# Turning half of the v tiles with VectorE and short transfer rows in a backbone on one Trainium2 core

## The chip, the cores and the metric

The kernel runs on one core of a Trainium2 chip. A core has four compute engines with a queue of instructions each: TensorE (PE) for matrix products and transposes into PSUM, VectorE (DVE), ScalarE (ACT) and GpSimd (POOL). SyncE (SP) only starts transfers. Sixteen DMA engines carry the transfers of all queues; in the profile those started by SP are queue q1 and those started by ACT are q10. The metric is the device time of one execution in microseconds (us), lower being better. Times are medians of several runs; profiles come from single executions.

## The reference

Two layers over 256 latent and 256 context tokens of width 1024, batch 1, in float32: a Conformer convolution module, then a bidirectional chunkwise mLSTM, each followed by an MLP with squared ReLU. The change lies in the features of the mLSTM:

```python
def mlstm_features(u, w_up, w_conv, b_conv, w_q, w_k, w_v, w_gate, b_gate, w_o, b_o):
    up = u @ w_up
    xm, z = up[..., :MLSTM_INNER], up[..., MLSTM_INNER:]
    xc = jax.nn.silu(dwconv(xm, w_conv) + b_conv)
    q, k, v = xc @ w_q, xc @ w_k, xm @ w_v
    gates = jnp.concatenate([q, k, v], axis=-1) @ w_gate + b_gate
    o = jax.nn.sigmoid(xm @ w_o + b_o)
    return xc, z, q, k, v, gates, o
```

`MLSTM_INNER` is 2048, split over 4 heads of 512. `v` is used twice: in the product with `w_gate`, and later, per head, as the right-hand side of the attention products, where tokens stand on the contracted dimension.

## The kernel before

Activations lie with channels on the 128 partitions and the 512 tokens (256 context, 256 latent) along the row, so a matrix of 2048 channels is sixteen tiles of 128x512. For accuracy every float32 product is done in three passes: a weight and an input are each split into a rounded high part and a low rest (`split`, lines 148-151: ACT casts the high part, `wh`; DVE subtracts it for the low part, `wl`), and `mm3` (lines 179-184) issues high x high, high x low and low x high.

Weights come as 1 MB loads on SP's queue into three buffers `raw` (`raw_load`, lines 141-144), two weight tiles in each. Four pairs of buffers `wh`/`wl` hold split tiles ahead of PE. `gemm_steps` (lines 224-281) walks over pairs of output tiles; after the last product of tile `m` it calls an epilogue.

The stage of v (lines 1207 to 1265) calls `gemm_steps(wv, range(8), xm, T, v_epi)`. The epilogue `v_epi(m, ps)` copies the product from PSUM to a tile `vt` on ACT and puts the rest of the work on a list, `late`; when an even `m` ends, `flush()` first runs what the two tiles before it have left. That rest is `v_out(m, vt)`:

- when `m % 4 == 3`, four gate products (`gate_acc`, line 1211) of that tile and the three before it, into 32 columns of PE each;
- four transposes of 128x128 on PE (line 1232) into a PSUM tile with the tag `ln`, so that tokens come to lie on the partitions;
- a copy from PSUM to a temporary `vk` of the tag `E` on ACT (line 1234), which has four buffers;
- one transfer of `vk` to a DRAM tensor `v_dr[head]`, issued by ACT (line 1235). `v_dr` holds 128 tokens on its first dimension, four blocks of tokens on the second and 512 channels on the third. `raw_load` fetches it back per head, after 1240 us in the profile.

Between the steps of this stage the kernel runs other work: `wgq_step` (lines 764-782) loads a 1 MB block of `wqT` and multiplies it with gate weights into 32 columns of PE (line 772); `ada_n2.step` (lines 408-430) loads a tile `ar` and scales and adds it on DVE (line 425); `xc_load` (lines 1245-1252) loads what the convolution wrote and splits it into `u` and `xc` tiles. After the stage a last `flush()` handles tiles 14 and 15, the pool of the stage is closed, and the products of the queries begin (lines 195 and 196), with `u` and `xc` as inputs and the tag `E` for each tile's sum (`joined`, lines 202-207).

The order of the instructions on each engine is fixed when the kernel is built: a scheduler takes them by priority, which is the order of the program, but lets a ready instruction of an idle engine go ahead. On the chip each engine works through its own list in that order and waits where data isn't there.

Of the kernel before, what the change touches and what calls it, by code (L numbers as in the profile page):

```python
# [14 lines left out]
P = 128  # L15
D = 1024
DT = D // P
E = 2048
# [52 lines left out]
def hybrid_kernel(ctx: ExitStack, tc: tile.TileContext, xT, vecs_d, wdw_d, ada0_w, ada_w, wg_d, pw1a, pw1, pw2, w1_0, w2_0,  # L71
                  w1_1, w2_1, up_x, up_z, wv, wo, bo_d, wk, wq, wqT, wdown, rows_d, out):
    nc = tc.nc
# [10 lines left out]
    def nm(s):  # L84
        uid[0] += 1
        return f"{s}_{uid[0]}"
# [3 lines left out]
    def tmp(tag, dt=F32):  # L90
        return tp.tile([P, T], dt, tag=tag, name=nm(tag), bufs={"E": 4, "S": 2, "L": 2, "F": 1}[tag])
# [8 lines left out]
    def psum(tag="mm"):  # L100
        return pp.tile([P, 512], F32, tag=tag, name=nm(tag), bufs={"mm": 3, "ln": 2, "fl": 1, "cv": 2}[tag])
# [1048 lines left out]
    v_dr = [dp.tile([P, 4, DH], F32, name=f"v_dr{h}") for h in range(H)]  # L1150
# [59 lines left out]
    def gate_acc(j, w, t, last=False):  # L1210
        nc.tensor.matmul(gps[32 * j:32 * j + 32, :], w, t, start=j not in seen, stop=last,
                         tile_position=(0, 32 * j), skip_group_check=True)
        seen.add(j)
# [4 lines left out]
    def v_epi(m, ps):  # L1218
        vt = B("vt").rearrange("p a b -> p (a b)")[:, :T]
        nc.scalar.copy(vt, ps)  # L1220
        vts.append(vt)
        if m % 2 == 0:
            flush()
        late.append(lambda: v_out(m, vt))

    def v_out(m, vt):
        if m % 4 == 3:
            for j in range(4):
                gate_acc(j, wgv[:, m - 3 + j, :], vts[m - 3 + j])
        tr = psum("ln")  # L1230
        for b in range(4):
            nc.tensor.transpose(tr[:, b * P:(b + 1) * P], vt[:, b * P:(b + 1) * P], ident)
        vk = tmp("E")
        nc.scalar.copy(vk, tr)
        nc.scalar.dma_start(v_dr[m // 4][:, :, (m % 4) * P:(m % 4 + 1) * P], vk.rearrange("p (b c) -> p b c", b=4))
# [755 lines left out]
```

## Time and profile before

| | before |
|---|---|
| time, median of 3 runs (lowest to highest) | 1673.76 us (1672.92 to 1674.23) |
| profiled execution: time, span | 1674.57 us, 1672.9 us |
| mean granted clock of PE | 0.998 |
| busy: PE, PE's weight loads, DVE, ACT | 99%, 82%, 62%, 44% of the span |
| stage of v in the trace | about 735 to 927 us |
| transfers from ACT to `v_dr` | 16 of 256 KB, median 4.1 us from issue to landing |
| queue q1 (SP), whole run | 56,080 packets, 285.44 MB, 48.5% of 16 engines |
| queue q10 (ACT), whole run | 17,712 packets, 14.72 MB, 2.6% of 16 engines |

A row of a group or of the timeline gives the line of the kernel, the engine, the operation, and what it writes and reads ("ln<-ident,vt"; numbers of buffers are left out). "x8" is a count, and "[9.75 <-DMA raw<-wv]" is the idle time before the instruction and what ended it. PEld are the weight loads of PE, which run beside its products; ACTq and SPq are the issuing of transfers by those queues. Matmuls are pipelined, so the duration of one is longer than the distance between two.

### The profile page before, as it was taken

What the parts mean: (1) busy time and instruction counts of PE and PEld (TensorE: products, weight loads), DVE (VectorE), ACT (ScalarE), POOL (GpSimd) and SP (SyncE); (2) the same over time, 40 slices, a digit from 0 to 9 for tenths busy, and PEclk for the clock granted to TensorE, in tenths of its full rate; (3) what the DMA queues carried; (4) which work ended last, traced back from release to release, by engine and by line L of the source; (5) the groups of instructions that cost most, each with busy time, mean ns of one, the idle gap of its engine ahead of it and who ended that gap; (6) DMA issues with size and microseconds to landing.
All of it is one profiled execution on the core that took longest, in us unless ns stands there. A gap on an engine that the chain in (4) does not pass through costs nothing. (4 is left out here: it accounts for less than half of the span.)

```text
span 1672.9 us, 22919 instructions
## 1 busy us (share of the span) xinstructions
PE 1660.0 (99%) x8928; PEld 1366.8 (82%) x8928; DVE 1034.3 (62%) x1877; ACT 744.0 (44%) x1196; POOL 14.3 (1%) x64
## 2 busy tenths in 40 slices
PE   9999999999999999999999999999999999999998
PEld 6665898888888998877788899888878888778887
DVE  6555895666635776752143653564389876786677
ACT  4313573232324476652232532442368654555453
POOL 0000000000000000000000000000000000000001
PEclk9999999999999999999999999999999999999999
DMA  9565213444424065556685753455375555675452
GB/s 356 202 215 207 88 71 114 151 135 139 142 101 151 1 210 187 183 195 248 254 271 168 262 175 120 136 205 170 133 246 192 193 210 211 249 272 190 182 186 92
DMA packets 73902, 301.63 MB, mean 180 GB/s; under 512 B 7519, under 2 KB 23683, under 8 KB 43969
## 3 DMA queue, kind: packets, MB, share of 16 engines
q1 hardware_dynamic: 56080, 285.44, 48.5%
q10 hardware_dynamic: 17712, 14.72, 2.6%
q8 instruction: 70, 1.15, 0.3%
q14 instruction: 40, 0.32, 0.1%
HBM read 284.37 MB, written 15.77 MB: 179 GB/s over the span
## 5 line engine op out<-in xcount | busy, mean ns | idle before, releaser
L150 DVE TENSOR_TENSOR wl<-raw,wh 128x1024 fp32r<-128x1024 f32 x344 | 418.7, 1221 | 275.7 <-ACT wh L149 273.2
L149 ACT CAST wh<-raw 128x1024 fp32r<-128x1024 f32 x344 | 359.3, 1052 | 509.6 <-PE mm L183 277.2
L183 PE MATMUL mm<-u,wh 128*128 128x512 f32 (+1 forms) x808 | 291.7, 361 | 0.2 <-DVE u L610 0.2
L180 PE MATMUL mm<-u,wh 128*128 128x512 f32 (+1 forms) x680 | 244.4, 360 | 0.1
L184 PE MATMUL mm<-u,wl 128*128 128x512 f32 (+1 forms) x680 | 241.4, 356 | 0.0
L183 PEld LDWEIGHTS mm<-u,wh 128*128 128x128 f32 x808 | 152.6, 189 | 23.1 <-issue 1.0
L180 PEld LDWEIGHTS mm<-u,wh 128*128 128x128 f32 x680 | 128.5, 189 | 25.7 <-issue 6.4
L184 PEld LDWEIGHTS mm<-u,wl 128*128 128x128 f32 x680 | 128.4, 189 | 18.8 <-issue 1.0
L211 PE MATMUL mm<-wh,xl 128*128 128x512 f32 x256 | 101.1, 395 | 0.0
L180 PE MATMUL mm<-xm,wh 128*128 128x512 f32 x256 | 101.0, 395 | 0.0
L212 PE MATMUL mm<-wh,xl 128*128 128x512 f32 x256 | 100.1, 391 | 0.0
L184 PE MATMUL mm<-xm,wl 128*128 128x512 f32 x256 | 99.7, 390 | 0.0
L213 PE MATMUL mm<-wl,xl 128*128 128x512 f32 x256 | 99.2, 391 | 0.1
L180 PE MATMUL mm<-hid,wh 128*128 128x512 f32 (+1 forms) x256 | 93.3, 364 | 0.0
L183 PE MATMUL mm<-hid,wh 128*128 128x512 f32 (+1 forms) x256 | 92.9, 363 | 0.0
L184 PE MATMUL mm<-hid,wl 128*128 128x512 f32 (+1 forms) x256 | 92.8, 363 | 0.0
L195 PE MATMUL mm<-x,wh 128*128 128x512 f32 x232 | 81.1, 398 | 0.0
L425 DVE SCALAR_TENSOR_TENSOR S<-ar,cs,S 128x512 f32<-128x512 f32 x56 | 40.8, 749 | 59.0 <-DMA ar<-ada_w 58.9
L183 PE MATMUL mm<-qq,wh 128*128 128x272 f32 x256 | 73.9, 289 | 0.0
L180 PE MATMUL mm<-qq,wh 128*128 128x272 f32 x256 | 73.5, 288 | 0.0
L184 PE MATMUL mm<-qq,wl 128*128 128x272 f32 x256 | 73.5, 288 | 0.0
L195 PE MATMUL mm<-u,wh 128*128 128x512 f32 x192 | 68.7, 399 | 0.0
(535 smaller groups left out, 3265.5 us busy)
## 6 DMA issues: line engine op xcount, KB each, us to landing
raw<-w SPq DMA_DIRECT2D x64, 1024.0 KB, 4.8
raw<-wo SPq DMA_DIRECT2D x32, 1024.0 KB, 4.8
raw<-ada_w SPq DMA_DIRECT2D x22, 1024.0 KB, 6.7
ar<-ada_w SPq DMA_DIRECT2D x80, 256.0 KB, 3.7
raw<-wv SPq DMA_DIRECT2D x16, 1024.0 KB, 7.1
raw<-wqT SPq DMA_DIRECT2D x16, 1024.0 KB, 6.2
raw<-wq SPq DMA_DIRECT2D x16, 1024.0 KB, 4.9
raw<-wk SPq DMA_DIRECT2D x16, 1024.0 KB, 4.9
```

The costliest lines, as they stand in the source:

```text
L149: c = nc.scalar.copy(hi, src)
L150: lastsub[0] = nc.vector.tensor_tensor(lo, src, hi.bitcast(F32), op=ALU.subtract).ins
L180: a = nc.tensor.matmul(ps, wh, xh, start=start, stop=False)
L183: nc.tensor.matmul(ps, wh, xl, start=False, stop=False)
L184: lastmm[0] = nc.tensor.matmul(ps, wl, xh, start=False, stop=stop).ins
L195: todo = [lambda s_, e_: nc.tensor.matmul(ps, wh, r[0], start=s_, stop=e_), lambda s_, e_: nc.tensor.matmul(ps[:, :n], wl, r[0][:, :n], st ...
L211: nc.tensor.matmul(ps, xh, wh, start=start, stop=False)
L212: nc.tensor.matmul(ps, xl, wh, start=False, stop=False)
L213: nc.tensor.matmul(ps, xh, wl, start=False, stop=stop)
L425: nc.vector.scalar_tensor_tensor(a, w, c, a, op0=ALU.mult, op1=ALU.add)
```

## The change

For odd `m`, the part of `v_out` behind the gate products is replaced. VectorE transposes `vt` within blocks of 32x32 into `vk`, so that each block is turned but stays at its place in the 4 x 16 grid of blocks. Four transfers issued by ACT, one for each 32 partitions, then write the blocks to where they belong in `v_dr`: each takes 32 partitions with 16 rows of 32 elements, that is 512 rows of 128 bytes, and the second and third dimension on the DRAM side put them at the right token block and quarter. The PSUM tile, the four transposes on PE, the copy on ACT and the one transfer with 512 rows of 512 bytes are not done for these tiles. Even tiles keep them.

```diff
@@ -1227,6 +1227,14 @@
         if m % 4 == 3:
             for j in range(4):
                 gate_acc(j, wgv[:, m - 3 + j, :], vts[m - 3 + j])
+        if m % 2:
+            vk = tmp("E")
+            nc.vector.transpose(vk, vt)
+            for q in range(4):
+                f0 = (m % 4) * P + 32 * q
+                nc.scalar.dma_start(v_dr[m // 4][:, :, f0:f0 + 32].rearrange("(q i) b j -> i b q j", i=32),
+                                    vk[32 * q:32 * q + 32, :].rearrange("i (b q j) -> i b q j", b=4, q=4))
+            return
         tr = psum("ln")
         for b in range(4):
             nc.tensor.transpose(tr[:, b * P:(b + 1) * P], vt[:, b * P:(b + 1) * P], ident)
```

## The prediction

> **What bounds the kernel now.** I read the page first, then the waits of PE alone, then the stretches around the v stage, and only then single instructions.
>
> ```profile
> span 1672.9 us, 22919 instructions
> ## 1 busy us (share of the span) xinstructions
> PE 1660.0 (99%) x8928; PEld 1366.8 (82%) x8928; DVE 1034.3 (62%) x1877; ACT 744.0 (44%) x1196; POOL 14.3 (1%) x64
> ```
>
> ```profile
> PE fl L342 <- DMA raw<-ada_w: 1.1, 2, 0.9
> ...
> PE mm L183 <- DVE u L610: 0.2, 1, 0.2
> ```
>
> These are the first and the last of the seven rows that the view of waits has for PE over the whole run; the longest is 1.1 us, so all seven together are under 8 us. The kernel is one long row of matrix products with hardly a gap. Two things follow. A matmul taken out anywhere shortens the run by the time until the next one could start, because nothing else ends later. And a delay on another engine costs nothing until PE has to wait for it; from then on it costs in full, since PE has no gap in which to catch up.
>
> ```profile
> 735.00:835.00 100.00, 100.00 (x511) 71.90 (x513) 25.05 (x26) 27.80 (x39) 0.00 (x0) 1.00 0.69 252
> 835.00:925.00 90.00, 90.00 (x430) 72.12 (x422) 39.01 (x59) 33.12 (x57) 0.00 (x0) 1.00 0.65 211
> 925.00:950.00 25.00, 25.00 (x141) 20.73 (x139) 15.83 (x28) 13.23 (x27) 0.00 (x0) 1.00 0.87 301
> ```
>
> The columns are length, then busy time of PE, PE's weight loads, DVE, ACT and POOL, then clock, DMA share and GB/s. The first two stretches are the v products, the third the start of the queries. In the v stage DVE and ACT work a quarter to two fifths of the time and the transfers two thirds. In the third stretch everything is fuller: DVE 63%, ACT 53%, transfers 87%. If the change hurts, I expect it there.
>
> **What the change removes from PE.** Sixteen tiles of v are turned, four transposes each; eight tiles lose theirs. They stand in two patterns. Where an even tile of the next group of four ends, the turns of both waiting tiles run together, eight in a row (four such runs; first and last):
>
> ```profile
> 764.99 1.03 PE L1232 MATMUL ln<-ident,vt 128*128 128x128 f32 x8
> 765.95 0.64 PE L772 MATMUL fl<-raw,wgq 128*32 128x512 f32 x4
> ```
>
> ```profile
> 917.44 1.03 PE L1232 MATMUL ln<-ident,vt 128*128 128x128 f32 x8
> 918.23 0.48 PE L180 MATMUL mm<-xm,wh 128*128 128x512 f32 x1
> ```
>
> From the first transpose to the next other instruction it is 0.79 us in the last run, 0.96 in the first, where the 32-column product after it starts later and will go on doing so. I take 0.79: half of it is 0.40 us, four times 1.6 us. In the other four places the gate products stand between the two tiles, and the odd tile's four transposes come behind them (first and last):
>
> ```profile
> 793.37 0.66 PE L1232 MATMUL ln<-ident,vt 128*128 128x128 f32 x4
> 793.95 0.64 PE L772 MATMUL fl<-raw,wgq 128*32 128x512 f32 x4
> ```
>
> ```profile
> 926.70 0.66 PE L1232 MATMUL ln<-ident,vt 128*128 128x128 f32 x4
> 927.11 0.36 PE L196 MATMUL mm<-u,wl 128*128 128x256 f32 x1
> ```
>
> That is 0.58 us once, where two 32-column products will now touch, and 0.41 three times: 1.8 us. The saving on PE is 1.6 + 1.8 = 3.4 us. With 0.96 in place of 0.79 for the two runs that end at a 32-column product it would be 3.6; that is the ceiling, because nothing else leaves PE.
>
> **What it adds elsewhere.** On ACT each odd tile loses one copy and one transfer issue, and gets four issues:
>
> ```profile
> L1234 ACT COPY E<-ln x16: 579/593/610, 768.2 to 927.4; 128x512 f32<-128x512 f32 x16
> ```
>
> ```profile
> L1235 ACTq DMA_DIRECT2D v_dr<-E x16: 520/521/1534, 768.8 to 928.0; - x16
> ```
>
> An old issue names 128 x 4 = 512 rows of 512 bytes, a new one 32 x 16 = 512 rows of 128 bytes, so I price it the same, 0.52 us when nothing disturbs it. Four are 2.1 us; less one copy (0.59) and one issue (0.52) that is 1.0 us more of ACT per odd tile, 8 us in 190. At the longest row, 1.53, it would be 6.1 - 1.1 = 5.0 us. On DVE comes one block transpose per odd tile, which this trace does not show. Nearest are operations over as many elements:
>
> ```profile
> L1198 DVE SCALAR_TENSOR_TENSOR E<-pad,vecs,E 128x512 f32<-128x512 f32 x12 | 9.0, 750 | 9.5 <-ACT E L1196 9.0
> ...
> L421 DVE TENSOR_SCALAR S<-ar,cs 128x512 f32<-128x512 f32 x2 | 1.0, 482 | 2.9 <-DMA ar<-ada_w 2.9
> ```
>
> Between 0.48 and 0.75 us; I take 0.6, as it has one input: 5 us of DVE in a stretch where it is idle for 126 of 190. This goes at nothing.
>
> The transfers: 8 x 512 = 4,096 packets of 512 bytes go, 8 x 2,048 = 16,384 of 128 bytes come. What one costs is read where that queue (q10, ACT's) was nearly alone, from 920 to 922 us, and how it shares with SP's weight loads (q1) from 802 to 804:
>
> ```profile
> q10 hardware_dynamic: 1031, 0.51, 85.2%
> ```
>
> ```profile
> q1 hardware_dynamic: 101, 0.70, 91.9%
> q10 hardware_dynamic: 101, 0.05, 8.5%
> ```
>
> 0.852 x 16 engines x 2 us / 1,031 packets is 26 ns each. By its bytes alone a 128-byte packet would take a quarter, 6.6 ns; I take 26, a price per packet, as the same queue to the same tensor is the nearest row. At 26 the change adds 12,288 x 26 ns / 16 = 20 us of transfer time to 190 us that are two thirds full, at 6.6 nothing. More important is the second pair: with work in both queues they take turns, one packet each, 101 against 101. A weight packet there takes 0.919 x 32 us / 101 = 291 ns, so a small packet in front of each costs the weights 9% at most, as in the run before. The small ones pile up and drain when the weights pause. The Trainium skill ("DMA: Bandwidth & Descriptors", Queues, rings and completion order) says an engine drains a whole packet, typically 9 to 17 descriptors, from one queue before it turns to the next. The equal counts are turns of single records and do not show such bundles; by them an odd tile's small packets, 2.5 us of transfer time at 26 ns, would all go ahead of the weights, and with the later issue (below) a load would be up to 0.7 us late at each of two places: a sum of 2 us in place of 3.4.
>
> **Cover in the middle of the stage.** ACT's casts of the weights stand behind the issues. The tightest place is the first pair:
>
> ```profile
> 768.81 1.31 ACTq L1235 DMA_DIRECT2D v_dr<-E  x2
> 770.16 1.05 ACT L149 CAST wh<-raw 128x1024 fp32r<-128x1024 f32 x1 [0.90 <-ACT E L1234]
> ```
>
> ```profile
> 772.50 0.33 SPq L143 DMA_DIRECT2D raw<-wv  x1
> ```
>
> ```profile
> 781.42 2.37 DVE L150 TENSOR_TENSOR wl<-raw,wh 128x1024 fp32r<-128x1024 f32 x2 [8.96 <-ACT wh L149]
> ```
>
> ```profile
> 786.40 0.39 PE L180 MATMUL mm<-xm,wh 128*128 128x512 f32 x1
> ```
>
> The cast at 770.16 frees the raw buffer for the load at 772.50; when that has landed, its two halves are cast and subtracted from 781.42 on (the first done near 782.6), and PE begins on it at 786.40. That is 3.8 us of cover. Five issues in place of two make the cast 1 to 2 us later; the transfer engines work off what is queued meanwhile, so the landing moves by that or less. Hidden; without cover it would be 1 to 2 us at each of two or three such places.
>
> ```profile
> L149 ACT CAST wh<-raw 128x1024 fp32r<-128x1024 f32 x30 | 30.9, 1050 | 86.3 <-DMA raw<-wv 43.8 <-PE mm L183 35.7 <-DVE S L425 4.4
> ```
>
> The 35.7 us in which these casts wait for PE lie almost all behind 835 us: there they are as far ahead as their four buffers let them, and a delay is hidden. ACT now also waits for DVE's transpose before the four issues, and casts stand behind that on ACT, as subtractions stand behind the transpose on DVE. But vt is there long before the flush, so the transpose can be done early, except for tile 15. Nothing is moved past SP's or POOL's queue.
>
> **Cover at the end of the stage.** Tile 15 has no such lead:
>
> ```profile
> 925.79 0.52 ACTq L1235 DMA_DIRECT2D v_dr<-E  x1
> 927.39 0.59 ACT L1234 COPY E<-ln 128x512 f32<-128x512 f32 x1 [1.63 <-PE ln L1232]
> 927.87 0.41 ACT L149 CAST xc<-raw 128x256 fp32r<-128x256 f32 x1
> 928.00 0.52 ACTq L1235 DMA_DIRECT2D v_dr<-E  x1
> 928.57 2.26 ACT L149 CAST xc<-raw 128x256 fp32r<-128x256 f32 x7 [0.28 <-ACT xc L149]
> ```
>
> ```profile
> 933.91 0.39 PE L195 MATMUL mm<-xc,wh 128*128 128x512 f32 x1
> ```
>
> The last xc cast ends at 930.8; PE takes the first xc at 933.9, so about 3 us of cover. The copy at 927.39 waited for PE's turn; DVE can do its turn earlier. So the four issues, 2.1 us, start about 0.7 us sooner than the one did, the casts end 0.5 to 1 us later, and PE arrives 0.4 us earlier: some 1.5 us of cover stay.
>
> **The sum.** The profiled execution took 1674.57 us, 1.67 around its span of 1672.9, and lies 0.81 above the median of 1673.76. 1674.57 - 3.4 is 1671.2; against the median, 1670.4. A measurement of this kernel tells about 0.2%, 3.35 us, from no change. The forecast lies on that bound.
>
> **The rivals.**
>
> *ACT is held at the end (slower), 0.27.* Tile 14's one and tile 15's four transfers put 5 x 32 = 160 packets on each of the 16 engines. The trace shows that ACT may run ahead of the engines by two: both issues of 768.81 were through at 770.12, and the next row (770 to 772) has no packet of q10 at all.
>
> ```profile
> q1 hardware_dynamic: 107, 0.75, 103.9%
> ```
>
> Whether it may run ahead by five, nothing shows. If 64 is the most, 96 packets per engine must go first, and weight loads keep the engines at 87% there. Taking turns at 291 + 26 ns, that is up to 30 us, in the pauses 2.5; halfway, near 12 us, is where loads dry up because ACT's casts no longer free their buffers. Of 12 us, 3 are covered and 1 replaced: PE waits about 8, net 8 - 3.4, 1678.4 us, and 1674.5 to 1681.5 for a hold of 8 to 15. It decides once ACT is held for over 5 us. Against it: the second of a pair of issues took at most 1.5 us.
>
> *Small rows are dear (slower), 0.13.* If a 128-byte write cost double, 53 ns, the change would add (16,384 x 53 - 4,096 x 26) / 16 = 48 us to the 190, the share would go to 0.92, the small packets would still be queued when the queries start, and the temporary that holds tile 15 would come free late, with ACT's copies of the queries behind it: 5 to 8 us of waits less 3.4, 1676 to 1678. The Trainium skill ("DMA: Bandwidth & Descriptors", Specifications) speaks against the change so: below 512 bytes a transfer engine reads, modifies and writes. No row here has a data row that short.
>
> *Cover runs out here and there (no difference), 0.10.* One to two microseconds at the first and third pair: 1671.5 to 1673.5. For it, the 3.8 us of cover; against it, the turn taking.
>
> **How the numbers follow.** The forecast, all hidden, has 0.50: 1670.4, itself 1669.8 to 1671.4. As 3.4 is so near 3.35 I split it, 0.30 faster and 0.20 within. With the rivals: faster 0.30, same 0.20 + 0.10 = 0.30, slower 0.27 + 0.13 = 0.40. The range from 1669.6 to 1681.0 leaves out the longest holds and a saving above the ceiling, together under 2 in 10.
>
> **What would show it.** Right: 32 transposes of v in place of 64, the pair at 871 replaced by four that take 0.4 us, PE's list of waits unchanged, four issues of about 0.52 us per odd tile, small packets at 7 to 26 ns. Wrong: a PE wait for xc, u or wh between 925 and 945; single issues of 2 us and more; weights that land some microseconds later after their issue than before; or a small packet at 50 ns or above.

## The result and the profile after

| | before | after |
|---|---|---|
| median (lowest to highest), 20 runs each | 1674.39 us (1672.92 to 1676.93) | 1676.90 us (1673.89 to 1679.91) |
| after / before | | 1.0015, 95% interval 1.0009 to 1.0022 |
| profiled execution: time, span | 1674.57, 1672.9 us | 1675.15, 1673.1 us |

The change costs 2.5 us where the forecast had a gain of 3.4. The time lies inside the range that was given, on the other side of no change. By the 0.2% that the prediction took as the least that can be told it would count as no change; over twenty runs each it is clear of noise. The profiled execution of after is one of its quicker ones, so what its trace shows is the lower end of the loss.

The head of the page of after:

```profile
span 1673.1 us, 22872 instructions
## 1 busy us (share of the span) xinstructions
PE 1658.8 (99%) x8896; PEld 1365.2 (82%) x8896; DVE 1038.6 (62%) x1885; ACT 737.1 (44%) x1188; POOL 14.3 (1%) x64
```

PE has 32 matmuls fewer (8896 against 8928), the transposes of eight tiles. They are gone; something gives the time back. The same stretches as before, and the one behind them (columns: length, PE, PE's weight loads, DVE, ACT, POOL, clock, DMA share, GB/s):

```profile
735.00:835.00 100.00, 100.00 (x507) 71.50 (x506) 28.22 (x30) 26.75 (x37) 0.00 (x0) 1.00 0.72 254
835.00:925.00 90.00, 90.00 (x416) 71.50 (x414) 38.42 (x58) 28.08 (x49) 0.00 (x0) 1.00 0.70 213
925.00:950.00 25.00, 24.12 (x135) 20.53 (x135) 19.05 (x33) 15.23 (x31) 0.00 (x0) 1.00 0.81 266
950.00:975.00 25.00, 22.67 (x124) 19.55 (x123) 15.44 (x26) 11.23 (x21) 0.00 (x0) 0.93 0.73 249
```

The stage of v itself is as full as before. PE has gaps only behind 925 us, 0.9 us in the third stretch and 2.3 us in the fourth, and in the fourth the clock is 0.93. PE's list of waits has two rows there that before has not:

```profile
PE mm L195 <- DVE E L206: 2.3, 1, 2.3
...
PE mm L195 <- ACT wh L149: 0.9, 2, 0.5
```

How these come about can be followed back from ACT's timeline at the end of the stage (start, length, line, and in brackets the idle time before):

```profile
922.51 2.67 ACTq L1235 DMA_DIRECT2D v_dr<-E  x4
925.23 0.71 ACT L149 CAST u<-raw 128x256 fp32r<-128x256 f32 x2 [3.10 <-DMA v_dr<-E]
925.85 2.56 ACT L149 CAST xc<-raw 128x256 fp32r<-128x256 f32 x8
928.31 1.04 ACT L149 CAST wh<-raw 128x1024 fp32r<-128x1024 f32 x1
929.25 0.20 ACT L149 CAST qq<-rk 128x16 fp32r<-128x16 f32 x1
929.36 1.04 ACT L149 CAST wh<-raw 128x1024 fp32r<-128x1024 f32 x1
```

Behind tile 15's four issues stand the last two casts of `u`, then those of `xc`, then the casts of the third and fourth tile of query weights. Before, the order was another: all casts of `u` and both of these `wh` stood ahead of tile 15's `vt` copy. The scheduler fixes the lists when the kernel is built, and with four issues where one stood it had ordered the work around them anew. The last cast of `u` before, and what follows it on DVE and on SP:

```profile
923.06 0.41 ACT L149 CAST u<-raw 128x256 fp32r<-128x256 f32 x1 [0.95 <-PE mm L183]
```

```profile
923.50 0.42 DVE L150 TENSOR_TENSOR u<-raw,u 128x256 fp32r<-128x256 f32 x1 [0.20 <-ACT u L149]
```

```profile
923.95 0.33 SPq L143 DMA_DIRECT2D raw<-wq  x1
```

And after:

```profile
925.66 0.76 DVE L150 TENSOR_TENSOR u<-raw,u 128x256 fp32r<-128x256 f32 x2 [3.08 <-ACT u L149]
```

```profile
926.45 0.33 SPq L143 DMA_DIRECT2D raw<-wq  x1
```

In both kernels the third load of query weights is issued 0.03 us behind the end of the last subtraction of `u` (923.92 and 926.42): it goes into the `raw` buffer from which `u` is cast. Tile 15's `vt` copy is at 924.69 before and 920.75 after, so the load goes out 0.7 us ahead of that copy before and 5.7 us behind it after. The larger wait comes 37 us later. VectorE's timeline there, and PE's, both of after:

```profile
962.50 0.75 DVE L425 SCALAR_TENSOR_TENSOR L<-ar,cs,L 128x512 f32<-128x512 f32 x1 [3.96 <-DMA ar<-ada_w]
963.17 0.42 DVE L206 TENSOR_TENSOR E<-mm,E 128x256 f32<-128x256 f32 x1
```

```profile
960.45 0.40 PE L195 MATMUL mm<-u,wh 128*128 128x512 f32 x1
960.68 0.28 PE L196 MATMUL mm<-u,wl 128*128 128x256 f32 x1
960.80 0.40 PE L195 MATMUL mm<-u,wh 128*128 128x512 f32 x1
961.03 0.28 PE L196 MATMUL mm<-u,wl 128*128 128x256 f32 x1
963.64 0.50 PE L195 MATMUL mm<-u,wh 128*128 128x512 f32 x1 [2.33 <-DVE E L206]
...
964.66 0.63 PE L195 MATMUL mm<-u,wh 128*128 128x512 f32 x1
965.09 0.41 PE L196 MATMUL mm<-u,wl 128*128 128x256 f32 x1
965.30 0.63 PE L195 MATMUL mm<-u,wh 128*128 128x512 f32 x1
```

An addition of `ada_n2` (line 425) waits 3.96 us for its tile `ar`; the sum of line 206, which PE needs, stands behind it on DVE, and PE loses 2.33 us. This is the fifth sum of the queries. In DVE's list seven additions of line 425 stand between tile 15's `vt` copy and this sum, and it starts 42.4 us behind that copy; before, five stand there, and it starts 34.5 us behind:

```profile
958.50 0.75 DVE L425 SCALAR_TENSOR_TENSOR L<-ar,cs,L 128x512 f32<-128x512 f32 x1 [1.00 <-DMA ar<-ada_w]
959.17 0.42 DVE L206 TENSOR_TENSOR E<-mm,E 128x256 f32<-128x256 f32 x1
```

After its wait PE runs slower for 3 us: a pair of products takes 0.64 us (964.66 to 965.30) where it took 0.35 before the gap (960.45 to 960.80).

The prices that the prediction had to bound can now be read. The four issues and DVE's turn:

```profile
L1235 ACTq DMA_DIRECT2D v_dr<-E x32: 581/672/4660, 769.9 to 924.5; - x32
```

```profile
L1232 DVE STREAM_TRANSPOSE E<-vt x8: 702/705/711, 769.1 to 921.4; 128x512 f32<-128x512 f32 x8
```

And the queues, from 923 to 925 us, where q10 is alone, and from 826 to 828 us (packets, MB, share of 16 engines):

```profile
q10 hardware_dynamic: 1583, 0.39, 83.8%
```

```profile
q1 hardware_dynamic: 116, 0.84, 99.8%
q10 hardware_dynamic: 115, 0.01, 4.7%
```

0.047 x 32 us / 115 makes 13 ns for a packet of 128 bytes. The Trainium skill ("DMA: Bandwidth & Descriptors", Specifications) has writes below 512 bytes as read, modify and write; here such a packet costs half of what the 512-byte packets cost (26 ns), not more, though by the byte that is twice as much.

### The profile page after: what moved, and what is told of

Its sections match the earlier page's. It is cut to its first block, busy times and chain, and to the rows that moved or that the text cites. A ratio compares the mean times of both kernels' runs of the same rounds, so it can differ in the third digit from the quotient of the medians.

```text
span 1673.1 us, 22872 instructions
## 1 busy us (share of the span) xinstructions
PE 1658.8 (99%) x8896; PEld 1365.2 (82%) x8896; DVE 1038.6 (62%) x1885; ACT 737.1 (44%) x1188; POOL 14.3 (1%) x64
## 4 chain that ended last, share of the span: by engine, by line
PE 94%; DVE 3%; DMA 2%; issue 1%; ACT 0%; ACTq 0%; SPq 0%; DVEq 0%
PE mm L180 17%; PE mm L184 17%; PE mm L183 17%; PE mm L195 6%; PE mm L211 4%; PE mm L213 4%; PE mm L212 4%; PE mm L196 3%; PE cv L211 2%; PE cv L213 2%; PE cv L212 2%; DMA ar<-ada_w 1%; PE fl L342 1%; PE ln L180 1%; PE cv L855 1%; PE ln L183 1%
```

## The experiments

Ratios are to the kernel before, run on the same chip beside it, with 95% intervals. Diffs are against the change unless it says otherwise. The first theories were: L, the loss is the order of ACT's list at the end of the stage; R, short rows slow the weight loads; H, ACT is held by the four issues wherever they stand; D, the transpose on DVE upsets something.

**The change once more.** 

> The change as it is, for a second profile beside the runs below. All theories: ratio 1.0015 (1.0009 to 1.0022). Theory L (order of ACT's list: the casts of the query weights that stood ahead of vt 15 now stand behind tile 15's four issues and the eight xc casts): PE waits of 2 to 7 us, all between 925 and 960 us, on wh or on DVE's sum of the queries. Theory R (128-byte rows slow the weight loads wherever they run): part of PE's waits before 925 us, on wh.

Measured: 1677.06 us, 1.0019 (1.0010 to 1.0028). Its profiled execution took 3.0 us of waiting for the sum of line 206, 2.0 us for `wl` and 0.9 us for `wh`, all between 925 and 970 us.

**One transfer for the four.**

```diff
-            for q in range(4):
-                f0 = (m % 4) * P + 32 * q
-                nc.scalar.dma_start(v_dr[m // 4][:, :, f0:f0 + 32]..., vk[32 * q:32 * q + 32, :]...)
+            nc.scalar.dma_start(v_dr[m // 4][:, :, (m % 4) * P:(m % 4 + 1) * P], vk.rearrange("p (b c) -> p b c", b=4))
```

> VectorE turns the odd tiles, but they are stored with one transfer of 512-byte rows as before (the 128-byte blocks stay at their old place, so v is not the reference's). Removes both the short rows and three of four issues; PE saves its 3.4 us. Theories L and R: 0.998 (-3.4 us), no PE wait between 925 and 960. Theory D (the transpose on DVE itself, or the removal on PE, upsets the order): 1.001 or more.

Measured: 1669.94 us, 0.9978 (0.9969 to 0.9987), no wait of PE between 925 and 975 us. Taking 32 transposes from PE is worth 3.7 us (1673.63 - 1669.94), and VectorE's turn hurts nothing. D falls.

**Transposes left on PE, four transfers for odd tiles** (against the kernel before).

```diff
+        vk3 = vk.rearrange("p (b c) -> p b c", b=4)
+        if m % 2:
+            for q in range(4):
+                f0 = (m % 4) * P + 32 * q
+                nc.scalar.dma_start(v_dr[m // 4][:, :, f0:f0 + 32], vk3[:, :, 32 * q:32 * q + 32])
+            return
```

> TensorE turns all tiles as before, but the odd tiles are stored with four transfers of 512 rows of 128 bytes in place of one. No saving on PE. In its list on ACT the casts of the query weights stand ahead of vt 15 and of tile 15's four issues, as before the change. Theory L: 1.000 (within 1 us of before), although 16,384 short rows move and ACT is held by 32 issues. Theory R: the change's loss of 5.9 us without its saving, 1.0035. Theory H (ACT is held by the issues, wherever its casts stand): 1.002 to 1.004.

Measured: 1675.94 us, 1.0015 (1.0006 to 1.0024), by another way than the change. Here one issue is held for 4.1 us in mid-stage with a cast of weights behind it. The next load of weights is issued when that cast's subtraction has ended, its casts wait 5.8 us for it, and behind them stands the copy of line 777 for which PE waits (ACT's timeline, then SP's, then PE's waits):

```profile
824.37 4.14 ACTq L1239 DMA_DIRECT2D v_dr<-E  x1
828.55 1.05 ACT L149 CAST wh<-raw 128x1024 fp32r<-128x1024 f32 x1 [7.14 <-issue]
...
835.92 1.99 ACT L149 CAST wh<-raw 128x1024 fp32r<-128x1024 f32 x2 [5.83 <-DMA raw<-wv]
837.82 0.58 ACT L777 COPY F<-fl 128x512 f32<-128x512 f32 x1
```

```profile
830.89 0.33 SPq L143 DMA_DIRECT2D raw<-wv  x1
```

```profile
PE fl L780 <- ACT F L777: 1.8, 1, 1.8
```

PE's clock is 0.50 from 840 to 842 us, and eight products from 838.96 to 842.36 us take some 1.5 us more than they do at full clock. So H is not empty: a group of four can cost where something urgent stands behind it. In the change this cast stands ahead of the issues (819.79 us), and its load goes out at 822.13 us.

**The change for tiles 1 to 11 only, and for tiles 13 and 15 only.**

```diff
-        if m % 2:
+        if m % 2 and m < 12:      # first kernel
+        if m % 2 and m > 12:      # second kernel
```

> The change for odd tiles below 12 only; 13 and 15 are turned by TensorE and stored with one transfer. Keeps six of eight turns' saving, 2.6 us, and three quarters of the short rows. Theories L and H (loss at the end of the stage): 0.9985 (-2.6 us). Theory R: loss 4.4 less 2.6, 1.001.

> The change for tiles 13 and 15 only; 0.8 us of saving. Theory L: the whole loss remains, PE waits of 3 to 6 us between 925 and 970: 1.0015 to 1.003. Theory R: a quarter of the loss of 5.9 less 0.8: 1.0004.

Measured: 1671.45 us, 0.9991 (0.9982 to 0.9999) without the last two, with no wait of PE between 925 and 975 us; 1679.65 us, 1.0034 (1.0021 to 1.0048) with them alone, with 4.3 us of waits for the sum and 0.9 for `wh`. All of the loss hangs on tiles 13 and 15; the other six give a gain.

**The four issues at a lower priority of the scheduler.**

```diff
             for q in range(4):
                 f0 = (m % 4) * P + 32 * q
-                nc.scalar.dma_start(...)
+                with tc.high_priority(-400):
+                    nc.scalar.dma_start(...)
```

> The whole change, its four issues per odd tile only given a lower priority, so that the scheduler puts each of them into a later gap of ACT's list: the casts of the query weights stand ahead of vt 15 again. Same instructions, same 128-byte rows, same issues. Theory L (order of ACT's list at the end of the stage): the PE saving shows, 0.998 (-3.5 us), no PE wait between 925 and 970. Theory R (short rows slow the loads): as the change, 1.0015 to 1.002. Theory H (ACT held by the issues, wherever they stand): 1.000 to 1.002.

Measured: 1670.68 us, 0.9980 (0.9972 to 0.9989). The same rows, bytes and issues, only at other places in ACT's list: R falls, and the change is worth what the forecast said, 3.6 us.

**The same four issues with rows of 512 bytes, and the issues on GpSimd's queue.**

```diff
-                nc.scalar.dma_start(v_dr[m // 4][:, :, f0:f0 + 32]..., vk[32 * q:32 * q + 32, :]...)   # short rows
+                nc.scalar.dma_start(v_dr[m // 4][32 * q:32 * q + 32, :, ...], vk[32 * q:32 * q + 32, :]...)  # first kernel
+                nc.gpsimd.dma_start(...)                                                               # second, short rows
```

> VectorE turns the odd tiles; four issues per tile, each of 32 partitions with 512-byte rows (128 rows), so no short rows and issues of about 0.33 us; the blocks stay at their old place, so v is not the reference's. Its list on ACT has one cast of the query weights behind vt 15 and the next behind the xc casts, like the change. Theory L: PE waits on the late cast, between 0.999 and 1.001, above the 0.998 of one transfer. Theories R and H: 0.998.

> The whole change with the four transfers issued by GpSimd in place of ACT. The 128-byte rows all move; ACT is not held and its casts of the query weights stand ahead of vt 15. Theories L and H: 0.998. Theory R: 1.0015 or more. If GpSimd is slow at issuing, tile 15's temporary comes free late and ACT's copies of the queries wait for it: 1.001 to 1.003, with ACT waiting for DMA v_dr.

Measured: 1671.23 us, 0.9982 (0.9973 to 0.9991), and 1671.65 us, 0.9985 (0.9976 to 0.9994). The first missed what I had expected. One of the two casts of query weights stood behind the casts of `xc`, as in the change, and it cost nothing; that put in doubt that these casts are what matters in the order. The issues of this kernel took 0.57 us and more in place of 0.33, so tile 15's four hold ACT for 2.67 us, as in the change. But all casts of `u` stand ahead of them, and the third load of query weights goes out together with tile 15's `vt` copy (920.23 and 920.24 us).

**The casts of query weights late, alone.** In the kernel before, and in the kernel with one transfer per odd tile, a copy of one column makes these two casts wait until they stand as in the change.

```diff
+        if after is not None:
+            nc.vector.tensor_copy(hi[:, 0:1], after)
         anchors.append(split(hi, lo, src))
...
+                late = xcs[12][0][:, 0:1] if w_ap is wq and (g, kh) == (0, 1) else None   # second kernel: vts[15][:, 0:1]
```

> The kernel before, with its transposes on TensorE and its single transfers; only the casts of the third and fourth tile of query weights are made to wait for the first cast of xc (a copy of one column on VectorE writes into their buffer first), so that in ACT's list they stand where the change put them: behind all eight casts of xc, the products of row rk between them. No group of four issues holds ACT. Theory O, the order alone costs: 1.0015 to 1.0035, with waits of PE for wh and, some steps on, for E of L206 between 925 and 970 us. Theory OH, the order costs only together with the two groups of issues that hold ACT for 2.7 us each: 0.9995 to 1.0006, no such waits over 0.5 us.

> Odd tiles turned by VectorE and stored with one transfer of 512-byte rows (v is not the reference's), and the casts of the third and fourth tile of query weights made to wait for tile 15's vt (a copy of one column on VectorE), so that they stand behind the eight casts of xc as in the change. One issue per odd tile in place of four. Theory O: the 4 us that this kernel gained without the late casts are lost again, 0.9998 to 1.0012. Theory OH: 0.9973 to 0.9987, as without the late casts.

Measured: 1674.57 us, 1.0006 (0.9997 to 1.0015), and 1669.44 us, 0.9971 (0.9960 to 0.9982). The second has all the gain although the two casts stand behind `xc` (ACT's timeline), and its third load of query weights goes out early (SP's):

```profile
923.35 2.56 ACT L149 CAST xc<-raw 128x256 fp32r<-128x256 f32 x8 [1.36 <-PE cv L1214]
925.81 1.05 ACT L149 CAST wh<-raw 128x1024 fp32r<-128x1024 f32 x1
```

```profile
920.90 0.33 SPq L143 DMA_DIRECT2D raw<-wq  x1
```

The late casts of query weights, my reading of L up to here, fall as the cause by themselves.

**Only the issues of tiles 13 and 15 at a lower priority, and every tile turned by VectorE.** The text of the first expectation speaks of tile 15 alone, but `m > 12` takes in tile 13 as well: in the trace all eight issues of the two tiles stand one by one, from 916.77 to 946.65 us.

```diff
+                with tc.high_priority(-400 if m > 12 else 0):     # first kernel
-        if m % 2:
+        if True:                                                  # second, with -400 for all issues
```

> The whole change; only the issues of tile 15 are put into ACT's list at a lower priority, those of tiles 1 to 13 stay as in the change with groups that hold ACT for 4.7 to 7.5 us. The casts of the query weights come ahead of the casts of xc again. Theory that all of the loss is at the end of the stage: 0.9974 to 0.9989, as with all issues at low priority. Rival, the holds in mid-stage cost a part: 0.9992 to 1.0008.

> All sixteen tiles turned by VectorE and stored with four transfers of 128-byte rows, all issues at low priority, so that PE has no transposes of v left. If the saving per tile is what the odd tiles gave (3.7 to 4.4 us for eight of them) and everything else stays hidden: 1666 to 1668 us, 0.995 to 0.9965. If doubling the issues to 64 holds ACT where a cast is due, or buffers of tag E come free late because their issues stand late: 0.9975 to 1.001, with waits of PE for wh, vt or u between 740 and 970 us.

Measured: 1670.07 us, 0.9978 (0.9969 to 0.9987), so the place of the issues of tiles 13 and 15 makes the loss, and the six groups of tiles 1 to 11, of which the first three hold ACT for 6.7 to 8.4 us here, none of it. Tile 15's issues alone were not run. And 1667.74 us, 0.9965 (0.9952 to 0.9977): the best of all, 6.1 us for sixteen tiles. It beats both kernels.

**The casts of `u` early, and late.** The first kernel is the change with its issues in place; only the split of `u` tiles 8 to 11 has a higher priority. In the second, one transfer per odd tile, the last two casts of `u` wait for a cast of `xc`.

```diff
+                with tc.high_priority(50 if m0 == 8 else 0):                   # first kernel, in xc_load
+                    split(ts[s][:, LO], ts[s][:, HI], rx[...])
...
+    u_parts = xc_load(8)                                                       # second kernel
+    xc_load(12)
+    u_parts(3, xcs[12][0][:, 0:1])
```

> The whole change, with tile 15's four issues of 2.7 us where the change has them and as many bytes and rows; only the split of u tiles 8 to 11 gets a higher priority, so that the last two casts of u stand ahead of tile 15's issues in ACT's list. Theory U: the loss comes from those two casts, since the third load of query weights goes into the buffer that they read, and waits for it. Then that load is issued at about the time of tile 15's vt copy in place of 5.7 us behind it, PE doesn't wait for E of L206, and the ratio is 0.9973 to 0.9990. Rival Q: the issues hold something else (the casts of xc, which still come behind them): 1.0005 to 1.0028.

> Odd tiles turned by VectorE and stored with one transfer of 512-byte rows (v is not the reference's), which gave 0.9978; here the last two casts of u wait for a cast of xc (a copy of one column on VectorE), so that they stand behind all casts of xc although one issue per tile holds ACT for 0.6 us only. Theory U: the third load of query weights is issued 4 to 7 us later than without, PE waits for E of L206 or wl between 930 and 970 us, and most of the gain is lost: 0.9995 to 1.0025. Rival Q: 0.9973 to 0.9985.

Measured: 1670.95 us, 0.9984 (0.9975 to 0.9993) with `u` early. Tile 15's issues hold ACT even longer here, and `xc` is cast later than in the change, yet all is well (ACT's and SP's timelines of this kernel):

```profile
919.46 1.02 ACT L149 CAST u<-raw 128x256 fp32r<-128x256 f32 x3 [3.59 <-DMA v_dr<-E]
...
922.14 4.68 ACTq L1235 DMA_DIRECT2D v_dr<-E  x4
926.86 2.56 ACT L149 CAST xc<-raw 128x256 fp32r<-128x256 f32 x8 [4.41 <-issue]
```

```profile
921.03 0.33 SPq L143 DMA_DIRECT2D raw<-wq  x1
```

DVE's list has changed with them. Five additions of line 425 stand ahead of the fifth sum in place of seven, and the sum starts 38.0 us behind tile 15's `vt` copy in place of 42.4, early enough for PE:

```profile
956.59 0.75 DVE L425 SCALAR_TENSOR_TENSOR L<-ar,cs,L 128x512 f32<-128x512 f32 x1 [2.89 <-DMA ar<-ada_w]
957.25 1.22 DVE L150 TENSOR_TENSOR wl<-raw,wh 128x1024 fp32r<-128x1024 f32 x1
958.39 0.42 DVE L206 TENSOR_TENSOR E<-mm,E 128x256 f32<-128x256 f32 x1
```

The later loads of query weights do not tell the two kernels apart: the fourth to the eighth go out 9.7, 11.3, 18.2, 23.0 and 27.8 us behind that copy here, and 9.2, 13.8, 18.8, 23.5 and 28.2 us in the change.

With `u` late: 1671.85 us, 0.9991 (0.9982 to 0.9999), less loss than expected. The delay came out smaller than meant, since the third load went out at 923.25 us, 1.4 us behind tile 15's `vt` copy and ahead of the late casts, so into another buffer. Single executions lie between 1670.11 and 1676.29 us; the profiled one, of 1674.78 us, has the change's wait at the change's place:

```profile
PE mm L195 <- DVE E L206: 2.9, 1, 2.9
```

So late casts of `u` can bring that wait without any group of issues, though not in every execution. Six additions stand ahead of the fifth sum here, as many as in the kernel with one transfer. The two medians differ by 0.0013, and their intervals overlap.

**Two buffers for `ar`**, with the change and with the kernel before.

```diff
-            w = adp.tile([P, 512], F32, tag="ar", name=nm("ar"))
+            w = adp.tile([P, 512], F32, tag="ar", name=nm("ar"), bufs=2)
```

> The whole change, with two buffers ar in place of one, so that the load for an addition of line 425 is issued before the addition ahead of it has ended. ACT's list at the end of the stage is the change's, with two casts of u behind tile 15's issues. Theory A, the loss is made at its last link, where the addition waits 4 us for ar ahead of the sum of line 206 that PE needs: against the kernel before with two buffers ar 0.9970 to 0.9988, and no wait of PE for E of L206 over 0.5 us between 940 and 980 us. Theory K, late query weights are enough whatever the additions do: 1.0003 to 1.0030 against that kernel.

> The kernel before with two buffers ar, the measure for the run with the change. The loads of ar and raw change places in SP's list in all stages that use ar: between 0.997 and 1.003 by either theory.

Measured: 1672.30 us, 0.9991 (0.9982 to 1.0000), and 1673.85 us, 1.0001 (0.9992 to 1.0010). The second buffer is worth nothing before and 4.8 us with the change (against 1677.06, measured on another chip). Seven additions still stand ahead of the fifth sum, but they wait 2.5 us for `ar` in place of 11.8, and the sum starts 35.4 us behind tile 15's `vt` copy. In PE's list only the first, smaller wait is left near the queries, with the two casts of `u` as late as ever:

```profile
PE mm L195 <- ACT wh L149: 0.9, 2, 0.6
```

Between the two medians the ratio is 0.9991 as well (1672.30 / 1673.85), 0.0003 above what theory A had given, which left out the 0.9 us for `wh`, and below all that K allowed; by the interval above, no change is just within reach.

## Why the prediction was wrong

**The saving on PE** was right: 3.4 forecast, 3.7 measured alone (one transfer), 3.6 with everything in it (low priority). All sixteen tiles give 6.1, a little less than twice that.

**The step that failed is "Cover at the end of the stage".** It took ACT's list as it was and set the four issues in the place of the one, and of what stands behind them it looked only at `xc`. For `xc` it held: the issues began 1.8 us behind tile 15's `vt` copy instead of 3.3 (922.51 - 920.75 against 928.00 - 924.69), the last `xc` cast ended at 928.4 instead of 930.8, and PE never waited for `xc`. But the list is made anew by the scheduler at each build, and it put two casts of `u` behind the issues. These free the buffer of the third load of query weights. The four issues took 2.7 us where 2.1 were priced; that size is not the point, since with `u` ahead of them 4.7 us cost nothing. The 1.5 us of cover that I counted were cover for the wrong work. With those casts DVE's list behind the stage changed too, at which the prediction did not look: two more additions of line 425 stand ahead of the fifth sum. PE's waits of 0.9 and 2.3 us, and its slower products behind the second, stand where the forecast had none.

**The sum after the fact.** The profiled execution of after: saving 3.7; waits 0.9 and 2.3; the slow pairs behind the second wait, seven steps from 963.64 to 967.74 us that take 4.1 us instead of 7 x 0.35 = 2.5, another 1.6. That is 4.8 against 3.7, a net loss of 1.1; its time is 0.6 above that of the profiled execution of before. The second traced execution of the change, of 1678.76 us, has waits of 5.9 us there; the median of 1676.90 lies between the two.

**The rival "ACT is held at the end"** named the right engine and the right place, and a sign of it came, the PE wait for `wh`. Its mechanism was not this one. It set the deciding point at a hold of over 5 us from packets that pile up; the hold was 2.7 us, and the kernel with the hold of 4.7 us is fast. What decides in these runs is which cast stands behind the issues. That 1676.90 us falls among the times of this rival (1674.5 to 1681.5) and of the next (1676 to 1678) is chance. That ACT can't run far ahead of the transfers is true: with weights on the engines, the first four groups took 4.7 to 7.5 us in mid-stage. My 1 to 2 us of delay there was too small by several times, and the conclusion "hidden" stood because the scheduler had put casts ahead of the issues; where it had not, in the kernel with the transposes left on PE, the third group cost PE 1.8 us and some clock. That is also the answer to the rival "Cover runs out here and there": not in the change, where PE has no wait between 735 and 925 us, but in that kernel.

**"Small rows are dear"** is refuted: 13 ns a packet, not 53 nor the 26 that I took, turn by turn with the weights (116 against 115), and the kernel at low priority moves them all and gains. At 13 and 26 ns the change adds (16,384 x 13 - 4,096 x 26) / 16 = 6.7 us of transfer time, a third of the 20 that I had; the shares of the two stretches of the stage (0.72 and 0.70 against 0.69 and 0.65) make 7.5. The bundles of 9 to 17 descriptors that the Trainium skill describes ("DMA: Bandwidth & Descriptors", Queues, rings and completion order) show in these counts no more than before.

**DVE's transpose**: 0.70 us, inside the bounds of 0.48 and 0.75, taken as 0.6; hidden as forecast.

**Two sums** of the prediction are off, without bearing on the result. An odd tile's 2,048 small packets at 26 ns are 3.3 us on sixteen engines; 2.5 is what comes on top of the old transfer. And halfway between 2.5 and 30 us is 16, not 12.

**What stays open.** Moving the casts of `u` ahead takes the loss away (0.9984), and a second `ar` buffer takes back 4.8 of some 7 us: the change lies at 1.0019, the change with two buffers at 0.9991, and the kernel with one transfer, which has the whole saving, at 0.9978. Of the 2 us or so that are left then, 0.9 is PE's wait for `wh`; the rest has no explanation. The traces speak for this path from `u` to PE: the scheduler, with `u` late, lets more additions go ahead of the fifth sum, and on the chip most of these wait for the one buffer. Seven stand there in all three traces with the full loss (the change twice, tiles 13 and 15 alone), four to six in the fast kernels with one buffer. But no run moved the additions alone, with `u` where the change has it, so how much of the 2.3 us is their order and how much the late third load is not shown.

## What to carry to other kernels

Where a scheduler fixes the lists, an edit that changes the number of instructions on one engine changes the order of the others around it; so compare the lists of both kernels first, ask of each piece of work that fell behind the new instructions which buffer it frees and who loads into it, and look in the other engines' lists for work that moved with it. Price a group of transfer issues by where it stands: a hold of 7 us cost nothing in mid-stage, and 2.7 us ahead of two small casts went with the loss of the whole gain. The cheapest mend was to lower the priority of the work that nobody waits for soon; then the idea was worth 0.2%, and 0.35% for all tiles.

## What the runs showed of the hardware

- A wait of PE of 1.8 us or more can cost more than itself. In three of the four waits of 2.3 to 3.0 us in these traces (the change twice, `u` late) the pairs behind it took 0.64 us in place of 0.35 for some 3 us, 1.4 to 1.6 us more, and with the transposes left on PE the same came behind a wait of 1.8 us, with a granted clock of 0.50. Behind waits of 1.3 and 1.4 us (tiles 13 and 15 alone, late casts in the kernel before) the clock stayed at 1.00. In the kernel with only tiles 13 and 15, a wait of 3.0 us had no such tail, so it depends on more than the length. The Trainium skill ("TensorE: Matmul & The Clock Gate", What's actually happening) has half clock after an idle window of about 3.4 us that runs freely; the traces show it behind gaps of 1.8 to 3.0 us, all shorter. Whether the free running is why one gap had no tail, no run here shows.
- 128-byte packets of the store to `v_dr` cost 13 ns each where 512-byte packets cost 26.
- ACT's issues for transfers of 512 packets of 128 bytes take 0.58 us as long as few are queued, and up to 4.7 us each (6.5 us in the kernel with `u` early) when several are queued behind busy transfer engines. Four issues of 128 packets of 512 bytes each were not held so: the longest took 1.17 us. Issued by GpSimd, the transfers of 512 small packets took 0.74 to 0.94 us each to issue, none held:

```profile
L1235 POOL DMA_DIRECT2D v_dr<-E x32: 739/739/944, 769.1 to 926.9; - x32
```
